# Output projection's weight pairs kept in DRAM between two token groups, and the post-mix norm over four token tiles at once

## The chip, the cores and the metric

The kernel runs on one core of a Trainium2 chip. The metric is the device time of one execution in microseconds (us), lower is better. The core's engines work side by side, each through its own queue in order: TensorE (PE) multiplies matrices, VectorE (DVE) and GpSimd (POOL) work elementwise, ScalarE (ACT) applies functions and copies, and SyncE (SP) issues the transfers (DMA) between DRAM and on-chip memory.

## The reference, cut to what matters

One layer of a decoder over 2048 tokens of width 1024: two groups of heads are computed from one input projection, normalised each, and sent through one output projection; then a residual step, a gated FFN and an embedding step.

```python
o_hg = rmsnorm(o_hg, hg_out_norm) * silu(hg)
o_sb = rmsnorm(o_sb, sb_out_norm)
mix = concatenate([o_hg, o_sb]) @ w_out
h = x + rmsnorm(mix, attn_post_norm)
u = rmsnorm(h, ffn_pre_norm)
gate, up = split(u @ w_gate_up)
y = (silu(gate) * up) @ w_down
h = h + rmsnorm(y, ffn_post_norm)
```

`rmsnorm(x, w)` multiplies each token's row by `(mean(x * x) + 1e-6) ** -0.5` and then by `w`.

## The kernel before

The 2048 tokens are four groups of 512 (`GT`), each of four tiles (`TT`) of 128 tokens. Every product is made of three matmuls in a rounded float32 format: each operand is split into a high part (a cast on ACT) and a low part (the operand less its high part, on DVE or POOL), and `mm3` (L220) adds high x high, high x low and low x high.

**Order of the work.** PE's instructions run in the order in which the program writes them; generators woven into each other by hand (`weave`) set that order. The other engines' queues are ordered by the framework's list scheduler, which takes the written order as priority but lets an instruction go ahead once its inputs are ready in its own model of time. Three things hold an instruction back: `pin(...)` puts it behind the instruction written last before it on the same engine; two instructions that write the same tile keep their order; and a tile of a pool with so many buffers (`bufs`) can be written only when an earlier tile of that pool is no longer used. DMA issues on SP wait, in order, for what they need.

**Output projections.** Groups 0 and 1 are projected one after the other by `out_proj(g)` (L652), groups 2 and 3 together by `out_pair` (L829), with seven products in place of eight. `out_proj` works in four quarters of 256 columns and two halves of the rows of `w_out`; each such block is one `dense_op` (L248) with two weight pairs, of two row blocks each. `weight` (L213) loads a raw tile of 256 KB (tile `wr`, four buffers), casts it to the high part (L207) and subtracts for the low part (L208, in turn on DVE and POOL); the pairs lie in a ring of three (`w`). A block is four steps of PE: the first pair is used in steps 1 and 3, the second in steps 2 and 4. Both groups load and split the same sixteen tiles of `w_out`. The results stand in eight `mix` tiles (four token tiles, two column halves each; L690, L692). Into `out_proj(0)` and the first part of `out_proj(1)` the ends of the attention (`attention`) and of the recurrence (`hgrn`: matmuls at L542 and L553, multiplications on POOL at L579 and on DVE at L581) are woven.

**After the projection.** `post_mix(g)` (L934) makes h and u of groups 0 and 1. For each token tile it loads x (L941), squares the two halves of mix on ACT with a sum over the row (L271, in `row_rstd`), makes the reciprocal root on POOL (sum L273, power L276), multiplies mix by it and by the norm's weights on DVE (L946), adds it to x (L947: first half DVE, second half POOL), stores h (L948), squares h the same way, makes the second reciprocal root and scales h with it into the mix tile (ACT, L953). Then, tile by tile, PE transposes the scaled tiles (L959), ACT multiplies by the next norm's weights (L963), and the result is stored (L965). All squares write their elements into one tile, `junk`, that nobody reads. The tiles of x and h come from a pool of eight (`xt`), which also serves the norm's weights `gb` (two), results of `out_pair` and other loads. `post_mix` gives way twenty times: twelve steps for the norm and eight for the transposes.

**How they are woven.** `post_mix(0)` runs beside `out_proj(1)`: its first twelve steps go three at a time before the PE steps 1, 3, 5 and 7, the transposes from before step 9 on. `post_mix(1)` runs beside `out_pair`: three steps before each of the PE steps 3, 5, 7 and 9, the transposes from before step 13 on. Each step of `out_pair` is one token tile of one product; products go in the order 1, 2, 6, 3, 7, 5, 4, four steps each. The operands of product 6 are made during product 2 (L880 to 884): `scaled` (L798, pinned), an add (L1099), and a split; operand 0 ahead of step 5, operands 1 and 2 ahead of step 6, operand 3 ahead of step 7. Loads for `out_pair` (L843 to 850, L897, L858, L861) run from the last blocks of `out_proj(1)` on; the weights of three of its products come as stored pairs (`wo_p`).

Of the kernel before, what the change touches and what calls it, by code (L numbers as in the profile page):

```python
# [8 lines left out]
F32 = mybir.dt.float32  # L9
# [6 lines left out]
P = 128  # L16
# [3 lines left out]
GT = 512  # L20
# [70 lines left out]
def hybrid_block(  # L91
# [32 lines left out]
    on_s = dram.tile([HH, P, GT], F32, tag="on_s", name="on_s")  # L124
    wo_s = [dram.tile([2, P, GT], F32, tag=f"wo_s{k}", name=f"wo_s{k}") for k in range(ND // 2)]
    wg_p = [[dram.tile([4, 2, P, GT], F32, tag=f"wg_p{i}{n}", name=f"wg_p{i}{n}") for n in range(2)] for i in range(2)]
    wo_p = [dram.tile([3, 2, P, GT], F32, tag=f"wo_p{k}", name=f"wo_p{k}") for k in range(ND // 2)]
    o_s = [[dram.tile([P, GT], F32, tag=f"o_s{g}_{i}", name=f"o_s{g}_{i}") for i in range(ND)] for g in range(NG)]

# [56 lines left out]
    def xt(name="xt"):  # L186
        return fb.tile([P, GT], F32, tag="xt", name=name, bufs=8)
# [25 lines left out]
    def weight(src):  # L213

        raw = wpool.tile([P, 512], F32, tag="wr", name="wr", bufs=4)
        nc.sync.dma_start(raw.rearrange("p (k n) -> p k n", k=2), src.rearrange("(k p) n -> p k n", p=P))
        wcount[0] += 1
        return split(wpool, "w", 3, raw, nc.vector if wcount[0] % 2 else nc.gpsimd)
# [26 lines left out]
                    yield None  # L245
        yield banks

    def dense_op(w_cols, act):  # L248

        ws = [weight(w_cols(kk)) for kk in range(0, HH, 2)]  # L250
        banks = []
        for i in range(2):
            banks.append(mm_bank())
            for kk in range(HH):
                mv = [t[:, kk % 2 * 256:(kk % 2 + 1) * 256] for t in ws[kk // 2]]
                for j in range(2):
                    mm3(banks[i][:, j * 256:(j + 1) * 256], cut(act[kk], 2 * i + j), mv,
                        kk == 0 and j == 0, kk == HH - 1 and j == 1)
                if kk == 1:
                    yield None  # L260
            yield banks[i]

    def row_rstd(halves, out=None, ss=None, shared=None, placed=lambda ins: ins):
        if ss is None:
            ss = const.tile([P, 2], F32, tag="ss", name="ss", bufs=8)
            for j, y in enumerate(halves):
                if j and shared is not None:
                    nc.vector.scalar_tensor_tensor(
                        shared, y, 1.0 / D, y, op0=ALU.mult, op1=ALU.mult, accum_out=ss[:, j:j + 1])
                else:  # L270
                    placed(nc.scalar.activation(junk, y, AF.Square, scale=ROOT, accum_out=ss[:, j:j + 1]))  # L271
        r = const.tile([P, 1], F32, tag="ssum", name="ssum", bufs=8)
        nc.gpsimd.tensor_scalar(r, ss[:, 0:1], ss[:, 1:2], EPS, op0=ALU.add, op1=ALU.add)  # L273
        if out is None:
            out = const.tile([P, 1], F32, tag="rstd2", name="rstd2", bufs=6)
        nc.gpsimd.tensor_tensor(out, r, neghalf, op=ALU.pow)  # L276
        return out
# [7 lines left out]
    def operand(pool, tag, bufs):  # L285
        return [pool.tile([P, GT], F32R, tag=tag + s, name=tag + s, bufs=bufs) for s in ("h", "l")]
# [365 lines left out]
    def out_proj(g, res):  # L652
        ops, acc = res["o"], res["oss"]
        r_hg, r_sb = [], []

        def sums(acc):
            b = bank("tr")
            for t in range(TT):
                nc.tensor.matmul(b[:, t:t + 1], acc[:, t * P:(t + 1) * P], ones1, start=True, stop=True)
            rr = const.tile([P, 2 * TT], F32, tag="rg", name="rg", bufs=2)  # L660
            nc.vector.tensor_copy(rr[:, 0:TT], hgss[:, g, :])
            nc.vector.tensor_copy(rr[:, TT:], b[:, 0:TT])
            nc.gpsimd.tensor_scalar(rr, rr, 1.0 / (HH * P), EPS, op0=ALU.mult, op1=ALU.add)
            nc.gpsimd.tensor_tensor(rr, rr, neghalf.to_broadcast((P, 2 * TT)), op=ALU.pow)
            r_hg.extend(rr[:, t:t + 1] for t in range(TT))
            r_sb.extend(rr[:, TT + t:TT + t + 1] for t in range(TT))

        sums(acc)
        mix = [[None, None] for _ in range(TT)]
        for quarter in range(4):  # L670
            half, o = divmod(quarter, 2)
            if o == 0:
                for t in range(TT):
                    mix[t][half] = ev(name="mix")
            for part in range(2):
                def src(k, part=part, c=quarter * 256):
                    r = (part * HH + k) * P
                    return w_out[r:r + 2 * P, c:c + 256]

                bank_no = 0  # L680
                for b in dense_op(src, ops[part * HH:(part + 1) * HH]):
                    if b is None:
                        yield
                        continue
                    for n in range(2):
                        t = 2 * bank_no + n
                        d = mix[t][half][:, o * 256:(o + 1) * 256]
                        bn = b[:, n * 256:(n + 1) * 256]
                        if part == 0:
                            nc.scalar.activation(d, bn, AF.Copy, scale=r_hg[t])  # L690
                        else:
                            nc.vector.scalar_tensor_tensor(d, bn, r_sb[t], d, op0=ALU.mult, op1=ALU.add)  # L692
                    bank_no += 1
                    yield
        res["mix"] = mix
# [238 lines left out]
    def post_mix(g, mix, tags, new):  # L934
        gb = [xt("gb") for _ in range(2)]
        for j in range(2):
            nc.sync.dma_start(gb[j], attn_post_norm[0:1][:, j * GT:(j + 1) * GT].to_broadcast((P, GT)))
        for t in range(TT):
            hs = [xt("h"), xt("h")]
            for j in range(2):  # L940
                nc.sync.dma_start(hs[j], x[g * GT + t * P:g * GT + (t + 1) * P, j * GT:(j + 1) * GT])  # L941
            r = row_rstd(mix[t])
            yield
            for j in range(2):
                d = mix[t][j]
                pin(nc.vector.scalar_tensor_tensor(d, d, r, gb[j], op0=ALU.mult, op1=ALU.mult))  # L946
                (nc.gpsimd if j else nc.vector).tensor_tensor(hs[j], hs[j], d, op=ALU.add)  # L947
                nc.sync.dma_start(h_s[g][t * P:(t + 1) * P, j * GT:(j + 1) * GT], hs[j])  # L948
                if j == 0:
                    yield  # L950
            r = row_rstd(hs)
            for j in range(2):
                nc.scalar.activation(mix[t][j], hs[j], AF.Copy, scale=r)  # L953
            yield
        for t in range(TT):
            for j in range(2):
                b = bank(tags[(2 * t + j) % len(tags)])
                for c in range(TT):
                    nc.tensor.transpose(b[:, c * P:(c + 1) * P], mix[t][j][:, c * P:(c + 1) * P], ident)  # L959
                e = new()  # L960
                for c in range(TT):
                    k = TT * j + c
                    nc.scalar.activation(  # L963
                        e[:, c * P:(c + 1) * P], b[:, c * P:(c + 1) * P], AF.Copy, scale=g_ffn[:, k:k + 1])
                nc.sync.dma_start(  # L965
                    u_s[g][TT * j:TT * (j + 1), :, t * P:(t + 1) * P].rearrange("k p t -> p k t"),
                    e.rearrange("p (k t) -> p k t", k=TT))
                yield

    def post_late(g):  # L970

        n = g - (NG - 2)
        for t in range(TT):
            rows = slice(t * P, (t + 1) * P)
            ss = const.tile([P, 2], F32, tag="ss", name="ss", bufs=8)
            for j in range(2):
                cs = slice(j * GT, (j + 1) * GT)
                m, h = load(h2_s[g][rows, cs]), load(x[g * GT + t * P:g * GT + (t + 1) * P, cs])
                gb = load(attn_post_norm[0:1][:, cs].to_broadcast((P, GT)))
                nc.vector.scalar_tensor_tensor(m, m, rows_m[n][t], gb, op0=ALU.mult, op1=ALU.mult)  # L980
                nc.gpsimd.tensor_tensor(h, h, m, op=ALU.add)
                nc.sync.dma_start(h_s[g][rows, cs], h)
                nc.scalar.activation(junk, h, AF.Square, scale=ROOT, accum_out=ss[:, j:j + 1])
                if j == 1:
                    row_rstd(None, rows_h[n][t], ss)
                yield
# [690 lines left out]
```

## Time and profile before

| | us |
|---|---|
| median of 3 runs | 2941.12 (2939.77 to 2944.24) |
| the profiled execution | 2940.09 |
| its span | 2938.3 |

Of the span PE is busy 2849.0 us, DVE 2114.5, ACT 1580.3 and POOL 1405.8.

A profile is one execution. A row of a timeline gives the start in us from the beginning of the span, the duration in us, the engine, the line of the kernel, the operation, output and inputs, and in brackets how long the engine had been idle before it and whom it waited for. A row of a window gives its bounds, its length and the busy us of each engine with its number of instructions; then the clock that TensorE was granted (1.00 is full), the mean busy share of the DMA engines and GB/s. A group of one line gives the count, busy us, mean ns, and the idle time before. For one line alone the three figures are the shortest, the middle and the longest duration in ns. A row of DMA issues ends with the size and the middle time from issue to landing. PEld is PE's load of the stationary operand.

### The profile page before, as it was taken

Reading aid. Unit: us, or ns where it says so; the run is one execution under the profiler, and the core shown is the slowest. Engines: PE = TensorE matmul, PEld = TensorE weight load, DVE = VectorE, ACT = ScalarE, POOL = GpSimd, SP = SyncE. Lnnn points to the kernel's source line nnn. Section 1 sums busy time; section 2 is a strip of 40 time slices with the busy share of each in tenths; the row PEclk is TensorE's granted clock in tenths of the full one; section 3 lists DMA queues with packets and bytes.
Section 4 is the critical chain, followed back from the end, with each engine's and each line's share of the span. In section 5 each row is a group of like instructions: output and inputs, shape, how many; then the busy total and the mean of one; then the engine's idle time right before and its main releaser. Section 6 shows DMA issues by size and latency. Waiting matters only on the chain. (4 is left out here: it accounts for less than half of the span.)

```text
span 2938.3 us, 51950 instructions
## 1 busy us (share of the span) xinstructions
PE 2849.0 (97%) x17796; PEld 2387.9 (81%) x17796; DVE 2114.5 (72%) x3051; ACT 1580.3 (54%) x3220; POOL 1405.8 (48%) x1384
## 2 busy tenths in 40 slices
PE   9999999999999999988999999999999999999999
PEld 8878888887788788886888878788888888888777
DVE  4776777778888777767877777665877765656785
ACT  5667657666676776675532434455433333545542
POOL 3345456545665667673433333455732121456653
PEclk9999999999999999999999999999999999999999
DMA  7886576457655554459986788877965555677975
GB/s 229 238 254 178 173 219 208 140 165 213 193 181 170 172 155 139 132 169 326 332 281 204 263 286 268 268 209 219 345 209 168 164 177 180 213 223 234 333 253 166
DMA packets 487561, 635.27 MB, mean 216 GB/s; under 512 B 45185, under 2 KB 275585, under 8 KB 487297
## 3 DMA queue, kind: packets, MB, share of 16 engines
q1 hardware_dynamic: 487296, 631.95, 68.4%
q8 instruction: 141, 2.31, 0.3%
q14 instruction: 124, 1.01, 0.1%
HBM read 459.29 MB, written 172.49 MB: 215 GB/s over the span
## 5 line engine op out<-in xcount | busy, mean ns | idle before, releaser
L1083 ACT CAST wh<-wr 128x512 fp32r<-128x512 f32 x592 | 347.2, 618 | 485.3 <-PE mm L222 97.0
L1084 POOL TENSOR_TENSOR wl<-wr,wh 128x512 fp32r<-128x512 f32 x256 | 370.4, 1454 | 425.4 <-ACT wh L1083 378.5
L452 POOL TENSOR_TENSOR a<-be,ring 128x512 f32<-128x512 f32 (+2 forms) x320 | 325.9, 1019 | 401.2 <-DVE ring L448 372.6
L1084 DVE TENSOR_TENSOR wl<-wr,wh 128x512 fp32r<-128x512 f32 x336 | 296.1, 889 | 173.6 <-ACT wh L1083 154.1
L221 PE MATMUL mm<-uh,wh 128*128 128x512 f32 x968 | 400.7, 414 | 6.2 <-DVE vv L365 3.6
L223 PE MATMUL mm<-uh,wl 128*128 128x512 f32 x968 | 380.1, 393 | 0.0
L222 PE MATMUL mm<-ul,wh 128*128 128x512 f32 x968 | 379.8, 392 | 0.0
L448 DVE TENSOR_TENSOR_SCAN ring<-z,ring,be 128x512 f32<-128x512 f32 x192 | 245.6, 1279 | 86.6 <-ACT z L434 80.8
L221 PE MATMUL mm<-wh,uh 128*128 128x256 f32 (+1 forms) x840 | 259.6, 309 | 2.2 <-DVE eb L351 2.2
L222 PE MATMUL mm<-wl,uh 128*128 128x256 f32 (+1 forms) x840 | 247.1, 294 | 2.3 <-POOL wl L1084 1.5
L223 PE MATMUL mm<-wh,ul 128*128 128x256 f32 (+1 forms) x840 | 246.6, 294 | 0.0
L433 ACT ACTIVATE be<-z 128x512 f32<-128x512 f32 (+2 forms) x320 | 171.3, 535 | 99.0 <-DVE z L431 60.8
L465 DVE TENSOR_TENSOR al<-tr,ah 128x512 fp32r<-128x512 f32 (+1 forms) x320 | 191.4, 598 | 41.5 <-ACT ah L463 39.9
L1084 POOL TENSOR_TENSOR wl<-s,wh 128x512 fp32r<-128x512 f32 x40 | 88.0, 2206 | 273.9 <-ACT wh L1083 245.5
L221 PEld LDWEIGHTS mm<-uh,wh 128*128 128x128 f32 x968 | 183.0, 189 | 41.7 <-issue 2.9
L223 PEld LDWEIGHTS mm<-uh,wl 128*128 128x128 f32 x968 | 182.2, 188 | 41.0
L207 ACT CAST wh<-wr 128x512 fp32r<-128x512 f32 x256 | 158.5, 619 | 100.9 <-PE mm L222 50.5
L463 ACT CAST ah<-tr 128x512 fp32r<-128x512 f32 (+1 forms) x320 | 167.8, 524 | 83.0 <-PE tr L460 81.4
L208 POOL TENSOR_TENSOR wl<-wr,wh 128x512 fp32r<-128x512 f32 x128 | 171.4, 1339 | 77.4 <-ACT wh L207 57.6
L222 PEld LDWEIGHTS mm<-ul,wh 128*128 128x128 f32 x968 | 183.0, 189 | 30.5
L460 PE MATMUL tr<-ident,a 128*128 128x128 f32 x1088 | 177.3, 275 | 17.6 <-POOL a L452 17.6
L427 PE MATMUL z<-kt,q 128*128 128x512 f32 (+3 forms) x640 | 188.2, 375 | 0.0
(387 smaller groups left out, 7585.3 us busy)
## 6 DMA issues: line engine op xcount, KB each, us to landing
wr<-in_w_gate_up_dram SPq DMA_DIRECT2D x292, 256.0 KB, 4.1
wr<-in_w_in_dram SPq DMA_DIRECT2D x224, 256.0 KB, 3.4
wr<-hid_s SPq DMA_DIRECT2D x154, 256.0 KB, 3.5
wr<-in_w_down_dram SPq DMA_DIRECT2D x110, 256.0 KB, 3.9
wr<-h_s SPq DMA_DIRECT2D x96, 256.0 KB, 4.5
wr<-wd_s SPq DMA_DIRECT2D x88, 256.0 KB, 3.2
kt<-k_s SPq DMA_DIRECT2D x80, 256.0 KB, 3.3
vt<-v_s SPq DMA_DIRECT2D x80, 256.0 KB, 3.2
```

The lines of the kernel that those rows point to most:

```text
L208: (lo_engine or nc.gpsimd).tensor_tensor(lo, src, hi.bitcast(F32), op=ALU.subtract)
L221: nc.tensor.matmul(o, l[0], r[0], start=start, stop=False)
L222: nc.tensor.matmul(o, l[0], r[1], start=False, stop=False)
L223: nc.tensor.matmul(o, l[1], r[0], start=False, stop=stop)
L427: nc.tensor.matmul(z[:, :n], st["q"][i][:, tb * P:(tb + 1) * P], ch["k"][:, :n], start=i == 0, stop=i == 1)
L433: nc.scalar.activation(be[:, :n], z[:, :n], AF.Sigmoid, scale=0.125)
L448: nc.vector.tensor_tensor_scan(r[:, o:o + n][:, ::-1], z[:, :n][:, ::-1], be[:, :n][:, ::-1], init, op0=ALU.mult, op1=ALU.bypass)
L452: nc.gpsimd.tensor_tensor(a[:, :n], be[:, :n], r[:, o + 1:o + n + 1], op=ALU.mult)
L460: nc.tensor.transpose(tr[:, tb * P:(tb + 1) * P], ch["a"][tb][:, sb * P:(sb + 1) * P], ident)
L465: nc.vector.tensor_tensor(lo[:, lo_c:], tr[:, lo_c:], hi[:, lo_c:].bitcast(F32), op=ALU.subtract)
L1083: nc.scalar.copy(hi, src)
L1084: lo_engine.tensor_tensor(lo, src, hi.bitcast(F32), op=ALU.subtract)
```

## The change

Two parts, with the code around them otherwise as it was.

`dense_op` is told where its pairs are kept and whether they are made already. In `out_proj(0)` each pair is stored to DRAM right after it is split (two stores of 256 KB); in `out_proj(1)` the pairs are loaded from there (two loads of 256 KB) in place of raw load, cast and subtraction.

`post_mix` keeps one tile of sums for four token tiles. Its first four steps square the mix tiles; one chain on POOL makes all four reciprocal roots. The next eight steps load one half tile of x each, make h (now in place, in the mix tile), store it and square it; behind the last one a second chain on POOL makes the four roots of h, and tile 0 is scaled. Each further tile is scaled between the transposes of the tile before. The number of steps is the same. Two pools of small tiles get four buffers in place of eight.

```diff
-    def dense_op(w_cols, act):
-
-        ws = [weight(w_cols(kk)) for kk in range(0, HH, 2)]
+    def dense_op(w_cols, act, keep_at, made):
+        ws = []
+        for kk in range(0, HH, 2):
+            if made:
+                pair = operand(wpool, "w", 3)
+                for t, d in zip(pair, keep_at[kk // 2]):
+                    nc.sync.dma_start(t.bitcast(F32), d)
+            else:
+                pair = weight(w_cols(kk))
+                for t, d in zip(pair, keep_at[kk // 2]):
+                    nc.sync.dma_start(d, t.bitcast(F32))
+            ws.append(pair)
...
-                for b in dense_op(src, ops[part * HH:(part + 1) * HH]):
+                for b in dense_op(src, ops[part * HH:(part + 1) * HH], wk_s[quarter][part], g == 1):
...
+        ss = const.tile([P, 2, 2, TT], F32, tag="sq", name="sq", bufs=1)
+
+        def square(n, t, j, y):
+            nc.scalar.activation(junk, y, AF.Square, scale=ROOT, accum_out=ss[:, n, j, t:t + 1])
+
+        def rstd4(n):
+            r = ss[:, n, 0, :]
+            nc.gpsimd.tensor_tensor(r, r, ss[:, n, 1, :], op=ALU.add)
+            nc.gpsimd.tensor_scalar(r, r, EPS, None, op0=ALU.add)
+            nc.gpsimd.tensor_tensor(r, r, neghalf.to_broadcast((P, TT)), op=ALU.pow)
+
+        def normed(t):
+            for j in range(2):
+                nc.scalar.activation(mix[t][j], mix[t][j], AF.Copy, scale=ss[:, 1, 0, t:t + 1])
+
         for t in range(TT):
-            hs = [xt("h"), xt("h")]
             for j in range(2):
-                nc.sync.dma_start(hs[j], x[g * GT + t * P:g * GT + (t + 1) * P, j * GT:(j + 1) * GT])
-            r = row_rstd(mix[t])
-            yield
+                square(0, t, j, mix[t][j])
+            if t == TT - 1:
+                rstd4(0)
+            yield
+        for t in range(TT):
             for j in range(2):
-                d = mix[t][j]
-                pin(nc.vector.scalar_tensor_tensor(d, d, r, gb[j], op0=ALU.mult, op1=ALU.mult))
-                (nc.gpsimd if j else nc.vector).tensor_tensor(hs[j], hs[j], d, op=ALU.add)
-                nc.sync.dma_start(h_s[g][t * P:(t + 1) * P, j * GT:(j + 1) * GT], hs[j])
-                if j == 0:
-                    yield
-            r = row_rstd(hs)
-            for j in range(2):
-                nc.scalar.activation(mix[t][j], hs[j], AF.Copy, scale=r)
-            yield
+                h, d = xt("h"), mix[t][j]
+                nc.sync.dma_start(h, x[g * GT + t * P:g * GT + (t + 1) * P, j * GT:(j + 1) * GT])
+                pin(nc.vector.scalar_tensor_tensor(d, d, ss[:, 0, 0, t:t + 1], gb[j], op0=ALU.mult, op1=ALU.mult))
+                (nc.gpsimd if j else nc.vector).tensor_tensor(d, h, d, op=ALU.add)
+                nc.sync.dma_start(h_s[g][t * P:(t + 1) * P, j * GT:(j + 1) * GT], d)
+                square(1, t, j, d)
+                if (t, j) == (TT - 1, 1):
+                    rstd4(1)
+                    normed(0)
+                yield
...
+                if j == 0 and t + 1 < TT:
+                    normed(t + 1)
                 yield
```

More of the change, by code (lines that the diff above doesn't have):

```diff
@@ L126, in hybrid_block @@
     wg_p = [[dram.tile([4, 2, P, GT], F32, tag=f"wg_p{i}{n}", name=f"wg_p{i}{n}") for n in range(2)] for i in range(2)]
+    wk_s = [[dram.tile([HH // 2, 2, P, GT], F32, tag=f"wk_s{q}{j}", name=f"wk_s{q}{j}") for j in range(2)] for q in range(4)]
     wo_p = [dram.tile([3, 2, P, GT], F32, tag=f"wo_p{k}", name=f"wo_p{k}") for k in range(ND // 2)]
@@ L264, in row_rstd @@
         if ss is None:
-            ss = const.tile([P, 2], F32, tag="ss", name="ss", bufs=8)
+            ss = const.tile([P, 2], F32, tag="ss", name="ss", bufs=4)
             for j, y in enumerate(halves):
@@ L271, in row_rstd @@
                     placed(nc.scalar.activation(junk, y, AF.Square, scale=ROOT, accum_out=ss[:, j:j + 1]))
-        r = const.tile([P, 1], F32, tag="ssum", name="ssum", bufs=8)
+        r = const.tile([P, 1], F32, tag="ssum", name="ssum", bufs=4)
         nc.gpsimd.tensor_scalar(r, ss[:, 0:1], ss[:, 1:2], EPS, op0=ALU.add, op1=ALU.add)
@@ L974, in post_late @@
             rows = slice(t * P, (t + 1) * P)
-            ss = const.tile([P, 2], F32, tag="ss", name="ss", bufs=8)
+            ss = const.tile([P, 2], F32, tag="ss", name="ss", bufs=4)
             for j in range(2):
```

## The prediction

> **What bounds the kernel now.** I read the page first: one core, TensorE (PE) busy in 97% of the span, so only idle or slowed PE can be won. (An execution is about 1.8 us longer than its span: 2940.1 us for the profiled one, 1.0 below the median of the runs.)
>
> ```profile
> span 2938.3 us, 51950 instructions
> PE 2849.0 (97%) x17796; PEld 2387.9 (81%) x17796; DVE 2114.5 (72%) x3051; ACT 1580.3 (54%) x3220; POOL 1405.8 (48%) x1384
> ```
>
> All that the change touches runs between 1114 and 1402 us, so next I cut that stretch into windows: the first projection (to 1244), the second (1249 to 1331), then the paired projection with the second post-norm beside it.
>
> ```profile
> core 0: us, PE busy (x) PEld busy (x) DVE busy (x) ACT busy (x) POOL busy (x), PEclk, DMA share, GB/s
> 1168.00:1244.00 76.00, 71.07 (x909) 63.90 (x908) 56.91 (x94) 50.76 (x111) 51.87 (x62) 1.00 0.39 121
> 1249.00:1305.00 56.00, 47.69 (x653) 42.88 (x651) 37.13 (x61) 45.49 (x116) 44.23 (x54) 1.00 0.52 169
> 1305.00:1331.00 26.00, 24.89 (x208) 24.44 (x208) 14.10 (x25) 14.44 (x36) 16.34 (x18) 1.00 0.69 230
> 1331.00:1353.00 22.00, 22.00 (x99) 17.84 (x97) 13.69 (x20) 10.81 (x23) 7.36 (x8) 1.00 1.05 385
> 1353.00:1378.00 25.00, 14.73 (x52) 10.57 (x52) 20.07 (x30) 14.93 (x37) 7.27 (x11) 0.73 0.76 257
> 1378.00:1402.00 24.00, 22.22 (x113) 18.13 (x111) 18.06 (x27) 19.04 (x49) 3.55 (x4) 1.00 0.86 281
> ```
>
> PE idles 8.3 + 1.1 = 9.4 us in the second projection and 10.3 us from 1353 to 1378, where the granted clock also fell to 0.73. At the pace of the window before (22.00 / 99 = 0.222 us each) those 52 matmuls need 11.6 us, not 14.73: another 3.1. So PE can win at most 13.4 us in the one place and 9.4 in the other, of 2941.
>
> Whom PE waits for, from its timeline:
>
> ```profile
> 1258.76 0.46 PE L542 MATMUL hg<-qp,ks 128*32 128x32 f32 x32 [1.58 <-POOL qp L579]
> ...
> 1269.60 0.60 PE L959 MATMUL tr<-ident,mix 128*128 128x128 f32 x4
> ...
> 1355.53 0.50 PE L221 MATMUL z<-wh,uh 128*128 128x512 f32 x1 [2.52 <-ACT uh L207]
> ...
> 1357.41 0.63 PE L223 MATMUL z<-wh,ul 128*128 128x512 f32 x1
> 1360.53 0.80 PE L221 MATMUL z<-wh,uh 128*128 128x512 f32 x1 [2.50 <-ACT uh L207]
> ...
> 1367.43 0.79 PE L221 MATMUL z<-wh,uh 128*128 128x512 f32 x1 [5.25 <-ACT uh L207]
> ...
> 1377.75 0.60 PE L959 MATMUL tr<-ident,mix 128*128 128x128 f32 x4
> ```
>
> The big stall is one block, the first of product 6, whose four operands (L880 to 884) come late, the last at 1367.4. Why shows in the timelines of SP, ACT and DVE there:
>
> ```profile
> 1356.07 0.95 SPq L941 DMA_DIRECT2D h<-in_x_dram  x2
> ```
> ```profile
> 1366.15 0.63 ACT L271 ACTIVATE junk<-h 128x512 bf16<-128x512 f32 x1 [1.66 <-POOL h L947]
> ```
> ```profile
> 1341.88 0.69 DVE L852 TENSOR_TENSOR ul<-wr,uh 128x512 fp32r<-128x512 f32 x1 [5.34 <-ACT uh L851]
> ...
> 1362.98 0.69 DVE L947 TENSOR_TENSOR h<-h,mix 128x512 f32<-128x512 f32 x1
> 1363.58 0.75 DVE L946 SCALAR_TENSOR_TENSOR mix<-mix,rstd,gb 128x512 f32<-128x512 f32 x1
> 1364.24 0.75 DVE L798 SCALAR_TENSOR_TENSOR wh<-wh,g_sb,acc 128x512 f32<-128x512 f32 x1
> 1365.03 1.63 DVE L1099 TENSOR_TENSOR wr<-wr,wh 128x512 f32<-128x512 f32 x1
> ```
>
> The last operand (L798, L1099, then a cast on ACT that stands behind the Square at 1366.15) is pinned on DVE behind token tile 2 of the post-norm (L946, L947). Tile 2 is late because its x could be loaded only at 1356, into buffers that tile 0 had held to its end. And since every Square writes the one tile `junk`, tile t+1 cannot be squared before tile t's h: four round trips through ACT, POOL, DVE, POOL and ACT stand in a row.
>
> **Part by part: the post-norm.** Squares (32), products (16), adds (16) and scalings (16) keep their number. On POOL 16 sums and 16 one-column powers go; 8 short operations and 4 powers of four columns come:
>
> ```profile
> L276 POOL TENSOR_TENSOR rstd<-ssum,neghalf x16: 552/560/577, 1242.1 to 1379.1; 128x1 f32<-128x1 f32 x16
> ```
> ```profile
> L783 POOL TENSOR_TENSOR rq<-rq,neghalf x2: 1022/1058/1093, 1139.4 to 1310.9; 128x4 f32<-128x4 f32 x2
> ```
>
> The powers alone fall from 16 x 0.56 = 9.0 us to 4 x 1.06 = 4.2, beside PE's work. What counts is the order. The four round trips become one; h is free again after its add; and the last operand of product 6 is pinned behind tiles 0 and 1 and half of tile 2 with no norm to wait for in between. The start stays where it is: the first product is pinned behind the operation at 1341.88, which waits for a weight's load. So I count DVE from that operation's dispatch, 1342.5, with the rows above (0.75 a product, 0.69 an add or split): tile 0, 2.2; operands 0 to 2 at 2.1 each, 6.4; two evictions, 1.4; tile 1 and half of tile 2, 3.6; operand 3 to its add, 1.4. That is 15.0, 1357.5. For evictions and splits that come in between and adds slowed to 1.63 I put 2.5: ready at 1360 instead of 1366.7. PE's block, which ends 1.4 us after its last operand, ends near 1361 instead of 1368.9: **-8** (bounds: -13.4, the whole of it, and 0, if DVE keeps today's order).
>
> New is a barrier. No tile is scaled before all four h are squared, so PE's transposes of tile 0 wait for tile 3. In the second post-norm PE now comes to them at 1377.75, then at 1369.8. The last x is issued, I take it, between 1356 (today's time for tile 2) and 1360; loads in this stretch take
>
> ```profile
> h<-in_x_dram SPq DMA_DIRECT2D x8, 256.0 KB, 4.6
> ...
> wh<-wo_p SPq DMA_DIRECT2D x6, 256.0 KB, 5.3
> ```
>
> 4.6 us, then come an add on POOL (1.4, by the 1371 ns of a like subtraction below), the Square with its read-out (0.8), POOL's power and two short ones (1.7), the scaling (0.6): 1365 to 1369. Just in time; **+1** for what those engines do in between (0 to +4).
>
> In the first post-norm the barrier stands before the transposes at 1269.60. Today tile 0 is ready there, and tile 3 far behind:
>
> ```profile
> 1265.87 1.36 DVE L581 TENSOR_TENSOR ks<-ks,tree 128x256 f32<-128x256 f32 x1
> ...
> 1282.48 1.77 DVE L946 SCALAR_TENSOR_TENSOR mix<-mix,rstd,gb 128x512 f32<-128x512 f32 x1 [1.25 <-POOL rstd L276]
> ```
>
> After the change tile 3 is written behind the step of the recurrence that leaves DVE at 1267.2. Three products and an add (2.9), the add on POOL (1.4), Square (0.8), POOL (1.7, and 1.5 for a neighbour in its queue), scaling (0.6): 1276.1, **+6.5** (0 if tile 3 slips ahead; +13 if it keeps today's 1282.5). Behind the waiting transposes in PE's order stand the dense blocks, attention and the recurrence; ACT's and DVE's evictions wait for those.
>
> **The weights' pairs.** The second projection loses 16 loads, 16 casts, 8 subtractions on DVE and 8 on POOL, and gains 32 loads; the first gains 32 stores. Lines of the second projection, grouped:
>
> ```profile
> L208 POOL TENSOR_TENSOR wl<-wr,wh 128x512 fp32r<-128x512 f32 x8 | 11.0, 1371 | 0.3 <-ACT wh L207 0.3
> ...
> L207 ACT CAST wh<-wr 128x512 fp32r<-128x512 f32 x15 | 9.2, 614 | 2.7 <-PE mm L223 2.3 <-ACT xt L963 0.3
> ```
>
> ACT is spared 16 x 0.61 = 9.8 us, POOL 11, DVE 8 x 0.69 = 5.5. PE gains only where it waits behind them: of its 9.4 us the 1.58 (POOL's multiplication for it queues with such subtractions and powers) and about as much in smaller pieces; the others also catch up while PE stands at the barrier. **-3.5** (-9.4 to 0).
>
> The stores cost SP 32 x 0.5 us (two issues in 0.95 above) over 130 us at a DMA share of 0.39. Each waits for its subtraction with the loads of attention and of the recurrence behind it in SP's queue, and those run ahead by a chunk: 0 (to +2; I see no way to a gain).
>
> The loads: the ring holds three pairs. Until now the raw tile lay ready, and cast and subtraction (0.61 + 1.37) followed the release of a pair; now a transfer does, and SP's later loads wait behind it. The second pair of a block has two of PE's steps, each 12 matmuls of 24.89 / 208 = 0.12 us and what is woven in: 2.9 us in the last block, about twice that while attention runs. By the 5.3 us of a kept pair that is 2.4 us short in each of the last two blocks, part of which the later stall takes up: **+1** (0 to +5). The Trainium skill ("DMA: Bandwidth & Descriptors", "Anatomy of one DMA — SWDGE (gpsimd) path") fits a fixed 2.0 us plus bytes / 436e3 on another issue path, an estimate of 2.6 us for 256 KB; by it this term is 0, and the 5.3 us here speak against it.
>
> On the clock: after a single gap of 2.52 us matmuls took 0.63 us at 1357.41. The Trainium skill ("TensorE: Matmul & The Clock Gate", Part 1) says that an idle window of about 3.4 us halves the clock. By the page, gaps cut below that would win the 3.1 us as well; by this row they need not, and I count none of it beyond the -8.
>
> Sum: -8 + 1 + 6.5 - 3.5 + 0 + 1 = -3 us: 2937.1 against the profiled execution, 2938 against the median.
>
> **Rivals.** *The barrier costs nothing*: both post-norms are through before PE arrives, -8 - 3.5 = -11.5, 2930. For it: DVE, ACT and POOL were 66, 81 and 79% busy from 1249 to 1305 and lose 26 us of work. Against it: tile 3's place in the written order.
>
> *The barrier bites*: tile 3 keeps today's pace, PE stands at the first transposes until 1282.5, +13, and the second post-norm gives 4 instead of 8: 2941 + 13 - 4 = 2950, slower. For it: today each tile takes 11 us there (three from 1249 to 1282.5). Against it: the round trips that made that are gone. It decides when the last Square of the first post-norm ends after about 1279.
>
> *The pairs come late*, and so this part does not relieve PE: +5 for the ring, the -3.5 gone, the rest as forecast, -8 + 1 + 6.5 + 5 = +4.5, 2945.6; 2 more on SP make it slower.
>
> **How the numbers follow.** The forecast gets 0.40, the rivals 0.28, 0.20 and 0.12. 0.2%, about what a measurement of this kernel can tell from no change, is 5.9 us. Faster: 0.28 and 0.05 of the forecast, 0.33. Slower: 0.20 and 0.03 of the late pairs, 0.23. Same: 0.44. The likeliest case alone gives 2933 to 2943; the range over all reaches past the free barrier to the biting one, 2928 to 2950.
>
> **What would show it.** Right: the waits for uh before product 6 near 1360 down to about 4 us in all; a wait of about 6 us at the first transposes of the first post-norm for the scaling on ACT; no casts of wh in the second projection; waits for a kept pair's DMA only in its last blocks. Wrong: no wait at those transposes (faster), one beyond 10 us or DMA waits in every block (slower).

## The result and the profile after

The changed kernel takes **2972.2 us** (2970.4 to 2977.1, four runs) against 2940.4 (2938.2 to 2944.2, four runs) for the kernel before: a ratio of 1.0108, interval 1.0096 to 1.0120. It is 32 us slower, where 3 us faster was forecast, and it lies outside the range.

The head of the page of the profile after:

```profile
span 2975.3 us, 51965 instructions
...
PE 2883.2 (97%) x17796; PEld 2397.7 (81%) x17796; DVE 2107.1 (71%) x3043; ACT 1571.2 (53%) x3204; POOL 1379.5 (46%) x1356
```

The engines that lost work show it: DVE 7 us less, ACT 9, POOL 26. PE, with the same 17796 matmuls, is busy **34 us longer**. So most of the loss is not PE waiting; it is PE working more slowly. (The profiled execution took 2977.07 us, 4.9 above its median.)

To see where, I cut both traces at five events that every version has: the first result of the first output projection (ACT writes `mix`), the first transposes of either post-norm (PE reads `mix`), the first `sg` of the FFN, and PE's first `mm<-ident,c` of the embedding step. Lengths are in us, with PE's idle time in brackets; they are differences of start times in the traces.

| from, to | before | after | difference |
|---|---|---|---|
| start, first `mix` | 1157.2 | 1158.9 | +1.7 |
| first `mix`, transposes of post-norm 0 | 112.4 (9.6) | 121.8 (16.0) | +9.4 |
| these, transposes of post-norm 1 | 108.2 (15.0) | 113.1 (16.7) | +4.9 |
| these, first `sg` | 61.0 (1.8) | 63.0 (2.4) | +2.0 |
| first `sg`, first `mm<-ident,c` | 621.0 (8.8) | 626.9 (3.8) | +5.9 |
| this, end | 878.5 (16.1) | 891.6 (13.3) | +13.1 |

16 us are lost inside the stretch that the change touches, **19 us behind it**, where no instruction was changed, and there PE idles less than before. The profiled executions differ by 37 us, 5 more than the medians. Two windows of the trace, after and then before, one in the changed stretch and one behind it (us, then busy us and number of instructions by engine; the last three figures are the granted clock, the DMA share and GB/s):

```profile
1246.00:1281.00 35.00, 23.36 (x282) 20.60 (x281) 24.48 (x35) 18.65 (x48) 22.22 (x23) 0.89 0.52 170
...
2200.00:2400.00 200.00, 200.00 (x871) 163.31 (x870) 140.81 (x203) 60.35 (x101) 44.58 (x31) 1.00 0.52 163
```
```profile
1246.00:1281.00 35.00, 29.57 (x384) 26.46 (x383) 25.23 (x41) 28.61 (x72) 28.20 (x36) 1.00 0.45 152
...
2200.00:2400.00 200.00, 200.00 (x884) 165.68 (x883) 143.42 (x208) 62.73 (x106) 46.78 (x33) 1.00 0.57 179
```

From 2200 to 2400 us PE is busy throughout, at the full granted clock in both, and starts 871 matmuls in place of 884: 229.6 ns each against 226.2. The clock is not it, nor the DMA share, which is lower after. The experiments below take this up. (The first rows, of the stretch that the change touches, come up again where the barrier is discussed.)

Inside the changed stretch, the waits of PE grouped (line, whom it waited for, us in total, times, longest):

```profile
PE z L222 <- ACT uh L208: 7.6, 1, 7.6
PE tr L985 <- ACT mix L961: 5.5, 1, 5.5
PE mm L222 <- DMA wh<-wk_s: 5.0, 2, 4.4
...
PE hg L563 <- DVE ks L591: 3.2, 1, 3.2
```

The first row is the stall before product 6, 10.3 us before, which was to shrink to about 4 us; the second is the barrier of the first post-norm; the third is the wait for kept pairs, in the last two blocks alone; the fourth is the recurrence waiting for a multiplication that stands on DVE behind two products of the post-norm. How the barrier forms can be read from the timeline: ACT's last Square of h, POOL's three operations, ACT's scaling, PE's transposes:

```profile
1277.42 0.61 ACT L951 ACTIVATE junk<-mix 128x512 bf16<-128x512 f32 x1
...
1279.88 4.40 ACT L961 ACTIVATE mix<-mix,sq 128x512 f32<-128x512 f32 x7 [1.76 <-POOL sq L957]
```
```profile
1278.20 0.20 POOL L955 TENSOR_TENSOR sq<-sq 128x4 f32<-128x4 f32 x1 [3.18 <-ACT junk L951]
1278.49 0.24 POOL L956 TENSOR_SCALAR sq<-sq 128x4 f32<-128x4 f32 x1
1278.82 1.04 POOL L957 TENSOR_TENSOR sq<-sq,neghalf 128x4 f32<-128x4 f32 x1
```
```profile
1280.66 1.12 PE L985 MATMUL tr<-ident,mix 128*128 128x128 f32 x4 [5.52 <-ACT mix L961]
```

### The profile page after: what moved, and what is told of

It is laid out like the page before. It is cut to its first block, busy times and chain, and to the rows that moved or that the text cites. A ratio compares the mean times of both kernels' runs of the same rounds, so it can differ in the third digit from the quotient of the medians.

```text
span 2975.3 us, 51965 instructions
## 1 busy us (share of the span) xinstructions
PE 2883.2 (97%) x17796; PEld 2397.7 (81%) x17796; DVE 2107.1 (71%) x3043; ACT 1571.2 (53%) x3204; POOL 1379.5 (46%) x1356
## 4 chain that ended last, share of the span: by engine, by line
PE 66%; DVE 5%; DMA 4%; POOL 3%; ACT 3%; issue 3%; SPq 0%; POOLq 0%; ACTq 0%; DVEq 0%
PE mm L222 8%; PE mm L223 8%; PE mm L224 8%; PE z L224 4%; PE z L223 4%; PE z L222 4%; PE tr L223 4%; PE tr L222 4%; PE tr L224 4%; PE tr L470 2%; PE z L437 2%; PE av L222 2%; PE av L223 2%; PE av L224 2%; DVE ring L458 1%
## 5 line engine op out<-in xcount | busy, mean ns | idle before, releaser
L1111 ACT CAST wh<-wr 128x512 fp32r<-128x512 f32 x592 | 347.3, 618 | 510.4 <-PE mm L223 98.2
L1112 POOL TENSOR_TENSOR wl<-wr,wh 128x512 fp32r<-128x512 f32 x256 | 365.9, 1436 | 446.2 <-ACT wh L1111 411.8
L458 DVE TENSOR_TENSOR_SCAN ring<-z,ring,be 128x512 f32<-128x512 f32 x192 | 245.6, 1279 | 86.3 <-ACT z L444 80.5
L208 ACT CAST wh<-wr 128x512 fp32r<-128x512 f32 x240 | 148.7, 620 | 99.0 <-PE mm L223 50.5
L209 POOL TENSOR_TENSOR wl<-wr,wh 128x512 fp32r<-128x512 f32 x120 | 160.3, 1336 | 77.5 <-ACT wh L208 56.0
L470 PE MATMUL tr<-ident,a 128*128 128x128 f32 x1088 | 178.4, 276 | 18.1 <-POOL a L462 18.1
```

The costliest lines, as they stand in the source:

```text
L458: nc.vector.tensor_tensor_scan(r[:, o:o + n][:, ::-1], z[:, :n][:, ::-1], be[:, :n][:, ::-1], init, op0=ALU.mult, op1=ALU.bypass)
L470: nc.tensor.transpose(tr[:, tb * P:(tb + 1) * P], ch["a"][tb][:, sb * P:(sb + 1) * P], ident)
L1111: nc.scalar.copy(hi, src)
L1112: lo_engine.tensor_tensor(lo, src, hi.bitcast(F32), op=ALU.subtract)
```

## The experiments

### The drift behind the changed stretch

**A suspicion.** Two pools of small tiles went from eight buffers to four. By the addresses in the programs each buffer takes 32 bytes of a partition: 8 x 32 = 256 less, and 64 more for the new tile of sums. So 192 bytes are gone, and the tiles behind them (those of the *left* side: the pool `fb`, the weights' pool, and later the left half of the FFN's operands) moved down by 192. The tiles laid out from the other end (the *right* half of the FFN's operands) stayed. Every large tile has rows of 2048 bytes, and before the change left and right tiles lay at the same place modulo 2048. Matmuls of the FFN and of the embedding step take operands from both sides. Theory A: this costs the drift. Theory B: the change's own instructions, transfers or clock do.

Four runs were to tell: the shift alone, the changed kernel without the shift, and (further below) the two parts of the change, each alone.

The shift alone, on the kernel before:

```diff
-            ss = const.tile([P, 2], F32, tag="ss", name="ss", bufs=8)
+            ss = const.tile([P, 2], F32, tag="ss", name="ss", bufs=5)
...
-        r = const.tile([P, 1], F32, tag="ssum", name="ssum", bufs=8)
+        r = const.tile([P, 1], F32, tag="ssum", name="ssum", bufs=5)
```

> The kernel before with nothing changed but two pools of small tiles, five buffers each in place of eight. Each buffer takes 32 bytes of a partition, so every tile behind them moves down by 192 bytes, as in the changed kernel, while the tiles that are laid out from the other end of the memory stay. Theory A (the slow drift after the changed stretch comes from where the operands of a matmul lie relative to each other): about +19 us against the kernel before, all of it after 1440 us, with late 128x512 matmuls started about 232 ns apart in place of 227. Theory B (the drift comes from the change's own instructions, from its transfers or from a clock that they leave lower): 0, within 3 us.

Measured: 2957.7 against 2939.7, **+18.0** (ratio 1.0060, 1.0045 to 1.0075). Up to the first `sg` the trace is 0.9 us later than that of before, at the end 18.7.

The changed kernel with its tiles put back:

```diff
-            ss = const.tile([P, 2], F32, tag="ss", name="ss", bufs=4)
+            ss = const.tile([P, 2], F32, tag="ss", name="ss", bufs=8)
...
-        r = const.tile([P, 1], F32, tag="ssum", name="ssum", bufs=4)
+        r = const.tile([P, 1], F32, tag="ssum", name="ssum", bufs=6)
```

> The changed kernel with the small pools given back 192 bytes (eight and six buffers in place of four and four), so that every tile lies where it lay before. Theory A: the 19 us after the changed stretch are gone, and about +13 us of the +32 are left (those of the changed stretch itself). Theory B: still about +32.

Measured: 2948.6, **+8.8** (1.0032, 1.0019 to 1.0045). 23 of the 32 us (31.8 less 8.8) went with an edit that changes no operation. Theory B has fallen for the drift; the 8.8 us that are left are the change's own. Between 2200 and 2400 us, the window of the shifted kernel before, and of the changed kernel put back:

```profile
2200.00:2400.00 200.00, 200.00 (x872) 163.62 (x871) 145.93 (x211) 62.72 (x107) 47.50 (x33) 1.00 0.55 174
```
```profile
2200.00:2400.00 200.00, 200.00 (x884) 165.74 (x883) 148.21 (x215) 63.35 (x106) 48.23 (x33) 1.00 0.57 179
```

872 and 884: the pace follows the addresses, with the work of the change or without it.

**Which property of the addresses?** Three more placements. First, both sides moved by 192 bytes: the pools with five buffers as in the shift alone, and an unused tile at the far end:

```diff
+    gap = ctx.enter_context(tc.tile_pool(name="gap", bufs=1, side="right"))
+    nc.vector.memset(gap.tile([P, 48], F32, tag="gap", name="gap"), 0.0)
```

> The kernel before with everything moved down together: the left tiles by 192 bytes (small pools of five buffers) and the right tiles by 192 bytes as well (an unused tile of that size at the far end of the memory). It computes the reference. Theory R (what counts is how left and right tiles lie relative to each other): 0 within 3 us, matmuls 227 ns apart late as in the kernel before. Theory S (what counts is where a tile lies in the memory): +18, as with the left side moved alone.

Measured: +1.3 by the medians (2939.5 against 2938.1; ratio 0.9997, 0.9988 to 1.0007). Theory R: the relative place counts.

The left side moved by 64 bytes (`ss` with six buffers in place of eight, nothing else):

> The kernel before with the left tiles moved down by 64 bytes alone (one small pool with six buffers in place of eight). Theory R, if any distance that is no multiple of a row slice slows the matmuls: about +18 as for 192 bytes. R, if the cost grows with the distance: +4 to +8. Theory S: one of the same, it does not tell them apart.

Measured: **+16.9** (1.0054, 1.0039 to 1.0069). The cost does not grow with the distance.

The left side moved by 512 bytes (`ss` and `ssum` with two buffers, `rstd2` with four in place of six, `rq` and `rg` with one in place of two):

> The kernel before with the left tiles moved down by 512 bytes alone (five small pools with fewer buffers, which may delay a norm somewhere by a few us ahead of 1440 us). Theory R with a period of 512 bytes (the slice of 128 columns that a matmul loads): no slow drift after 1440 us, 227 ns apart. Theory R with a period of 2048 bytes (a tile's row): a drift of the size of the 192 bytes', about +18.

Measured: +1.9 (1.0006, 0.9996 to 1.0016), no drift. The windows of these three, in the same order:

```profile
2200.00:2400.00 200.00, 200.00 (x884) 165.60 (x883) 139.69 (x205) 62.70 (x105) 44.48 (x33) 1.00 0.55 175
```
```profile
2200.00:2400.00 200.00, 200.00 (x870) 163.03 (x869) 144.15 (x212) 62.03 (x104) 46.04 (x32) 1.00 0.57 177
```
```profile
2200.00:2400.00 200.00, 200.00 (x884) 165.62 (x883) 141.27 (x206) 63.30 (x106) 46.18 (x34) 1.00 0.56 176
```

So a distance between the two sides of 0 or 512 bytes is free, 64 and 192 cost 17 and 18 us. If the cost repeats with a period that divides 512 bytes, the period is over 64; 128 and 256 were not tried. Setting each matmul record beside the program's list of matmuls gives the side of its two operands. Mean distance of the starts of 128x512 matmuls after 1460 us, in ns (distances under 300 alone):

| moving operand, stationary operand | before | both by 192 | left by 512 | left by 192 | left by 64 |
|---|---|---|---|---|---|
| left, left | 227.0 | 227.0 | 227.0 | 228.4 | 231.5 |
| left, right | 227.0 | 227.0 | 227.0 | 229.4 | 233.1 |
| right, left | 226.9 | 226.9 | 226.8 | 233.2 | 229.4 |
| right, right | 227.0 | 226.9 | 226.9 | 231.6 | 227.8 |

Matmuls whose two operands lie on one side are slowed as well, so it is not simply the distance of the two operands of one matmul. What collides with what (the next weight load, writes of the other engines) these runs do not show. The Trainium skill ("SBUF — State Buffer", "SBUF: two separate sides") says that, of the engines, only DVE and GpSimd contend, and that PE's port never waits on anyone. These runs show no wait at a port, so they leave that sentence open; what they show is that the same matmul takes 227 or 233 ns by where tiles lie. And they show it for the stage behind 1440 us alone. Ahead of it, where other pools lie on the right, the 128x512 matmuls whose operands both lie in the weights' pool start 230.2 to 230.9 ns apart on the mean in all five kernels of this table.

### The changed stretch: which part costs what

Only the stored pairs, all tiles where they lay (the diff's first two parts and the pools with eight buffers):

> Only the stored pairs of the output weights, on the kernel before, with all tiles where they lay. Theory A with the rows of the changed kernel: +4 to +8, the waits for kept pairs in the last two blocks of the second projection (0.6 and 4.4 us there) less what the spared casts and subtractions win. Theory B (the drift is of the pairs' making): +15 to +25, with a slow drift after 1440 us.

Measured: -0.6 (2939.2 against 2939.7; ratio 0.9996, 0.9987 to 1.0006). The rows of its waits:

```profile
PE z L222 <- ACT uh L208: 7.1, 2, 5.6
PE hg L552 <- POOL qp L589: 5.0, 6, 1.8
PE mm L222 <- DMA wh<-wk_s: 4.3, 2, 3.9
```

The ring's price is there, 4.3 us, and is given back elsewhere: up to the transposes of post-norm 0 PE idles 8.0 us in place of 9.6, and the stall before product 6 is 5.6 where before had 10.3 (of the 7.1 above and the 11.9 below, 1.5 and 1.7 fall at a later block):

```profile
PE z L221 <- ACT uh L207: 11.9, 4, 5.2
```

Only the post-norm over four tiles, all tiles where they lay (`post_mix` of the changed kernel; `ss` with six buffers, which makes up for the new tile):

> Only the post-norm over four token tiles, on the kernel before, with all tiles where they lay (one of the small pools with six buffers, which makes up for the new tile). Theory A with the rows of the changed kernel: +5 to +12, mostly the wait of about 5.5 us at the first transposes of the first post-norm, with the stall before product 6 not much smaller than the 10 us of before. Theory B (the drift is of the post-norm's making): +20 or more, with a slow drift after 1440 us.

Measured: **+9.7** (2949.4; 1.0034, 1.0022 to 1.0047). The two parts together, -0.6 + 9.7 = 9.1, agree with the 8.8 of the changed kernel with its tiles put back. All of the 9.7 is lost before the first transposes (122.4 us from the first `mix` in place of 112.4; the two lengths behind are 108.8 and 61.5, as before within 1.0). And the stall before product 6, 10.6 us in place of 10.3, has **not** shrunk:

```profile
PE z L221 <- ACT uh L207: 10.6, 2, 8.8
PE tr L975 <- ACT mix L951: 7.8, 1, 7.8
```

Were fewer buffers of the sums a cost of their own? The changed kernel with four buffers, and an unused tile of 192 bytes behind them:

```diff
+    gap = ctx.enter_context(tc.tile_pool(name="gap", bufs=1))
+    nc.vector.memset(gap.tile([P, 48], F32, tag="gap", name="gap"), 0.0)
```

> The changed kernel as it is, its small pools with four buffers too, and an unused tile of 192 bytes behind them, so that all else lies where it lay before. Theory A (the addresses alone): as the version with more buffers, about +9 against the kernel before. Rival (fewer buffers of the sums delay the norms and cost a part of it): between +12 and +15.

Measured: +12.1 (2950.2 against 2938.1; 1.0045, 1.0029 to 1.0060). This interval and that of the version with more buffers overlap, so whether the buffers cost 3 us or nothing stays open. With the shift's 18.0 it gives 30.1 of the 31.8.

### Why the stall stayed, and whether the barrier is the barrier

In the post-norm alone, SP issued the loads of x for tile 1 and half of tile 2 at 1361 us, the rest at 1370:

```profile
1361.41 1.66 SPq L962 DMA_DIRECT2D h<-in_x_dram  x3
...
1370.02 1.35 SPq L962 DMA_DIRECT2D h<-in_x_dram  x3
```

The change writes each load in the step that adds it; before, a tile's loads were written a step or two ahead. So I moved them up:

```diff
+            fetch(*divmod(t, 2))
             for j in range(2):
                 square(0, t, j, mix[t][j])
...
-                h, d = xt("h"), mix[t][j]
-                nc.sync.dma_start(h, x[g * GT + t * P:g * GT + (t + 1) * P, j * GT:(j + 1) * GT])
+                h, d = xs[2 * t + j], mix[t][j]
...
+                if t + 2 < TT:
+                    fetch(t + 2, j)
                 square(1, t, j, d)
```

> The post-norm over four token tiles alone, all tiles where they lay, with x loaded four half tiles ahead (one in each of the steps that square mix, then one behind each add) in place of in the step that adds it. Theory X (the stall before product 6 stayed because the loads of x were issued at 1361 and 1370 us, behind SP's other work): that stall falls from 12 us to 4 to 6, the wait at the first transposes of 6 to 8 us stays, and the whole is +2 to +4 against the kernel before. Rival (DVE's own queue of products, adds and splits keeps the last operand late): the stall stays near 12, and the whole near +10.

Measured: 2951.0, +11.3 (1.0039, 1.0023 to 1.0054). The waits of PE now:

```profile
PE tr L983 <- ACT mix L951: 7.9, 1, 7.9
PE z L221 <- DMA h_s<-c: 5.1, 1, 5.1
...
PE z L221 <- ACT uh L207: 1.3, 2, 1.0
PE z L223 <- DVE ul L208: 1.3, 1, 1.3
```

Those before product 6 fell to 6.7 us in all, from 10.6 (the last three rows, less 1.0 of the one for `uh`, which falls at a later block), and the length between the first transposes of the two post-norms to 105.2 from 108.8. So theory X is right in sign, too large in size, and nothing of it shows in the whole.

In the post-norm alone it is DVE that delivers the last operand late. From the first product of the post-norm, where the forecast let DVE start, 22.5 us of the kernel before and of the post-norm alone (which runs 10 us later here):

```profile
1342.50:1365.00 22.50, 14.66 (x56) 10.37 (x54) 19.63 (x29) 13.02 (x32) 7.52 (x11) 0.81 0.94 339
```
```profile
1352.50:1375.00 22.50, 12.66 (x54) 9.64 (x52) 21.68 (x32) 8.56 (x21) 4.70 (x3) 0.86 0.93 335
```

DVE went from 87% to 96% busy. The last operand's add began 20.8 us after the start in place of 22.5 (1373.27 less 1352.5, and 1365.03 less 1342.5) and ended after 22.5 us in place of 24.2; the forecast had 17.5. The groups of DVE's lines there say with what:

```profile
L963 DVE SCALAR_TENSOR_TENSOR mix<-mix,sq,gb 128x512 f32<-128x512 f32 x7 | 5.0, 743 | 0.0
L964 DVE TENSOR_TENSOR mix<-h,mix 128x512 f32<-128x512 f32 x4 | 3.7, 921 | 0.1
...
L1114 DVE TENSOR_TENSOR wr<-wr 128x512 f32<-128x512 f32 x3 | 2.0, 681 | 0.0
```

Freed of its waits, the post-norm put seven products there (5.0 us), not the five that are written ahead of that operand, and three adds (the fourth of the row starts behind the operand's), one of them of 1.63 us. Three subtractions for a later product (L1114, 2.0 us), which stood there before as well, were not in the forecast's count. The idle gaps between the round trips were filled, not removed. The operand's add in the post-norm alone, then with x loaded ahead:

```profile
1373.27 1.75 DVE L1117 TENSOR_TENSOR wr<-wr,wh 128x512 f32<-128x512 f32 x1
```
```profile
1372.32 0.69 DVE L1125 TENSOR_TENSOR wr<-wr,wh 128x512 f32<-128x512 f32 x1
```

With x loaded ahead DVE starts at 1354.92 and has only the five products and three adds in front, and this add ends 18.1 us after the start: DVE's part of the forecast came about there. What kept PE waiting for most of its 6.7 us was the third operand, which DVE had ready at 1368.7. The row of 5.1 us above names a store; what came just before PE's start at 1371.73 was ACT's cast of that operand. It stood in ACT's queue behind a Square of h, which waited for an add on POOL, and that add took 5.32 us where the forecast had 1.4 (why, these runs do not show):

```profile
1365.09 5.32 POOL L970 TENSOR_TENSOR mix<-h,mix 128x512 f32<-128x512 f32 x1 [6.22 <-DVE mix L969]
```
```profile
1370.45 0.63 ACT L941 ACTIVATE junk<-mix 128x512 bf16<-128x512 f32 x1 [5.27 <-POOL mix L970]
...
1371.08 0.60 ACT L207 CAST uh<-wr 128x512 fp32r<-128x512 f32 x1
```

Now the barrier. The same version, but each tile's second root made by itself, and the tile scaled at once:

```diff
-                if (t, j) == (TT - 1, 1):
-                    rstd4(1)
-                    normed(0)
+                if j == 1:
+                    r = ss[:, 1, 0, t:t + 1]
+                    nc.gpsimd.tensor_scalar(r, r, ss[:, 1, 1, t:t + 1], EPS, op0=ALU.add, op1=ALU.add)
+                    nc.gpsimd.tensor_tensor(r, r, neghalf, op=ALU.pow)
+                    normed(t)
```

> As the version with x loaded ahead, and each token tile's second reciprocal root made by itself behind its two squares, and the tile scaled at once, so that no tile waits for tile 3; the first reciprocal roots are still made for four tiles at once. If the barrier is what the first transposes wait for: their wait of 6 to 8 us goes, and the whole is 6 to 8 us less than with x loaded ahead alone, which by theory X makes -2 to -6 against the kernel before. Rival (tile 0 is late in itself, behind the recurrence's operations on DVE): the wait stays over 4 us.

Measured: 2938.0, -1.7 (0.9998, 0.9986 to 1.0010): **13 us less** than with the barrier, and no difference from the kernel before. The wait at the first transposes is gone from the list, and they come 114.5 us after the first `mix` in place of 122.4. That is 7.9 of the 13. The profiled executions differ by 7.0 more between `sg` and the embedding step, which the edit does not touch; over all versions with left and right tiles in line that length runs from 614.7 to 621.7 us, so the barrier is shown to cost 7.9, not 13. The hoped-for -2 to -6 did not come.

Last, the place in DVE's queue. With PE's order kept, the second post-norm's twelve steps are written behind the operands of product 6, once in the kernel before and once in the version by tile:

```diff
-    weave(op, 1)
-    weave(op, 4, (pm, 3 * TT, 0))
+    weave(op, 4)
+    weave(op, 1, (pm, 3 * TT, 0))
```

> The kernel before with the first twelve steps of the second post-norm written behind the operands of product 6: ahead of step 9 of the paired projection all at once, in place of three each ahead of steps 3, 5, 7 and 9. PE's order is the same. Theory D (the stall of 12 us before product 6 is the place of its operands' operations in DVE's queue, behind the post-norm's): PE's idle time between the second post-norm's first... transposes of the first post-norm and the FFN falls by 6 to 9 us of 12, and the whole is -6 to -11, unless the second post-norm's four round trips, now begun some 10 us later, are late for their transposes (then up to +10 there, and the whole between -3 and +5). Theory L (the operands wait for their loads or for PE, not for DVE): no change, within 3 us.

> The version with the first roots for four tiles, x loaded ahead and the second roots by tile, and with the second post-norm's twelve steps written behind the operands of product 6, as in the other kernel of this call. Theory D: the stall before product 6 falls from about 9 us of idle PE to 2 to 4, tile 0 is in time for its transposes since it waits for no other tile, and the whole is -6 to -11 against the kernel before. Theory L: no change, about -2.

Measured: 2938.4 and 2940.9 against 2939.9 (0.9995, 0.9986 to 1.0004; and 1.0002, 0.9994 to 1.0011). The timeline of PE from 1335 to 1440 us with its waits, in the kernel before so edited, has three, none of them before product 6, where the kernel before stood at 1355, 1360 and 1367:

```profile
1366.24 0.96 PE L959 MATMUL tr<-ident,mix 128*128 128x128 f32 x4 [2.13 <-ACT mix L953]
...
1381.21 0.66 PE L959 MATMUL hg<-ident,mix 128*128 128x128 f32 x4 [0.44 <-ACT mix L953]
1390.90 0.79 PE L221 MATMUL z<-wh,uh 128*128 128x512 f32 x1 [6.75 <-ACT uh L207]
```

And in the version by tile one wait is left, at the transposes:

```profile
1379.51 1.12 PE L985 MATMUL tr<-ident,mix 128*128 128x128 f32 x4 [11.97 <-ACT mix L951]
```

Theory D is right on the mechanism (the stall came from the place of the post-norm's operations ahead of the operands') and wrong on the gain: 10 us of waiting became 9 or 12 us of waiting at the next thing that DVE, ACT and POOL have to deliver. No version here beats the kernel before by more than the measurement can tell.

## Why the prediction was wrong

| term | forecast | measured |
|---|---|---|
| stall before product 6 | -8 (-13.4 to 0) | 0: PE's waits there 10.3 us before, 10.6 with the post-norm alone (5.6 with the pairs alone, 7.6 with both parts) |
| barrier, second post-norm | +1 | 0: no wait for the scaling there |
| barrier, first post-norm | +6.5 (0 to +13) | PE's idle time to there +6.4 (9.6 to 16.0), with slower matmuls +9.4; with the post-norm alone +8.4 and +10.0 |
| pairs: relief, stores, ring | -3.5 + 0 + 1 = -2.5 | -0.6 (ratio 0.9987 to 1.0006, -3.8 to +1.8 us: the forecast lies inside) |
| two pools with four buffers: tiles moved by 192 bytes | no term | +18 |

**The step that failed is the sum itself**: "Sum: -8 + 1 + 6.5 - 3.5 + 0 + 1 = -3". It has no term for the two small pools, whose buffers stood in the diff and were costed neither as buffers nor as 192 bytes of a layout. That is 18 of the 32 us, shown from both sides: added to the kernel before, +18.0; taken from the changed one (with buffers given back), -23.0. Without it the change still costs 8.8 us where -3 was forecast, and the first four rows say where. The prediction's list of what would show it wrong looked only into the changed stretch; and its bound "only idle or slowed PE can be won" was applied to gains, not to a loss at 100% busy.

**The second is the size of the -8.** "For evictions and splits that come in between and adds slowed to 1.63 I put 2.5: ready at 1360": the last add was to end 17.5 us after DVE's start, and in the post-norm alone it ended after 22.5, because a queue ordered by readiness filled the gaps that the removed waits left. With x loaded ahead it ended after 18.1, and PE still waited 6.7 us, because the third operand's cast stood on ACT behind an add of 5.32 us on POOL: the sum counted DVE alone. The bound of 0 ("if DVE keeps today's order") was the truth for PE, though for another reason. The edit that did remove the stall shows that it was not there to be won: the next wait was as long.

**Right** was the barrier as a mechanism and in its place. The last Square ended near 1278.0; less the 1.7 us by which the trace ran late, that is before the 1279 from which the biting barrier was to decide, so the forecast's own case came about, with 5.5 us of wait in the place where "about 6" was named. That the wait came out so near is in part luck: by the same trace the scaled tile came 2.9 us later than the 1276.1 of the forecast (1280.66 less 1.7), and PE came to the transposes 3.8 us later than the 1269.60 of before (1280.66 less 5.52 and 1.7). What was not in the forecast: the granted clock fell to 0.89 there, and PE was busy 3.0 us longer with the matmuls up to there (105.8 us in place of 102.8). The longest gaps of PE in that window were 1.6, 1.3, 3.2 and 5.5 us. The Trainium skill ("TensorE: Matmul & The Clock Gate", Part 1) gives an idle window of about 3.4 us as the trigger; the version by tile, whose longest gap there was 2.89 us, still showed 0.95 from 1246 to 1281 us, so here again less than that was enough.

**Right** too: the kept pairs waited for their DMA in the last two blocks alone (0.6 and 4.4 us), the stores cost nothing that shows, and the relief of ACT, POOL and DVE about paid for the ring.

What stays open: about 2 to 5 us of the 32 that the parts do not add up to, among them what fewer buffers cost; why unaligned sides slow a matmul; and why one add on POOL took 5.32 us.

## What to carry to other kernels

A change of a small tile's buffers is a change of every address behind it: list the addresses before and after, and keep large operands that work together at the same place modulo 512 bytes, as before here (pad if need be); other distances than 64, 192 and 512 bytes were not tried. When a late trace is uniformly slower at 100% busy and full clock, look at the layout, not at the schedule. And a wait removed in front of an engine that is 87% busy was worth little here: ask what that engine will do with the gap, and who waits next; batching over tiles saves small operations but makes the first tile wait for the last.

## What the runs showed of the hardware that I had not expected

- The distance between 128x512 matmuls depends on where left and right tiles lie relative to each other: 227 ns at 0 and 512 bytes, up to 233 at 64 and 192, at a granted clock of 1.00 throughout. Over the last 1500 us that is 17 to 18 us.
- It cannot be seen in the clock, in PE's busy share or in any wait; the number of PE's instructions in a window of fixed length (884, 872, 870) and the distance of their starts show it.
- Adds of 128x512 on POOL, 1.26 to 1.74 us in the post-norm alone, took up to 5.33 us in two of the versions with x loaded ahead (`norm_early_x`, `norm_by_tile`).
- Loads of 256 KB of kept pairs took 3.3 and 3.7 us in the second projection, where 5.3 was assumed from a busier place:

```profile
wl<-wk_s SPq DMA_DIRECT2D x13, 256.0 KB, 3.3
wh<-wk_s SPq DMA_DIRECT2D x13, 256.0 KB, 3.7
```
